# Block sums of two right sides made by accumulating transfers: one Strassen-Winograd trunk layer on one Trainium2 core

## Chip, core and metric

The kernel runs on 1 core of one Trainium2 chip. The metric is the device time of one execution in microseconds (us). TensorE is called PE, VectorE DVE, ScalarE ACT, GpSimd POOL and SyncE SP. POOL and SP also issue the transfers.

## What is computed

One layer of a trunk on 1024 frames of width 1024, all in float32: an input projection, two gated mixers, their two output projections, a third output projection `w_o` into the residual, and a gated feed-forward block.

```python
merged = (sigmoid(gate_a + gate_bias[0]) * (y_a @ w_out_a)
          + sigmoid(gate_b + gate_bias[1]) * (y_b @ w_out_b))
x = x + merged @ w_o
h = rmsnorm(x, ln2_g)
x = x + (silu(h @ w_ffn_gate) * (h @ w_ffn_up)) @ w_ffn_down
return rmsnorm(x, final_g)
```

## The kernel before, in words

**Products.** Every large product is tiled by Strassen-Winograd: a `Pair` is two 128-row output tiles, and its right side is cut into row pairs (two 128-row tiles each, four of them for a width of 1024) and into frame halves H0 and H1 of 512. With a = `y[2q]` and b = `y[2q+1]`, row pair q has the four blocks a.H0 (B11), a.H1 (B12), b.H0 (B21) and b.H1 (B22). Seven products replace eight; each needs a block, or a sum of blocks, of both sides (`PRODS`, line 38). The right sides are called forms: B11, T1 = B11 - B12, T2 = B22 + T1, B21, T3 = B12 - B22, T4 = B21 - T2 and B22.

**Float32 by three products.** Each form, and each left block or sum, is split into a high part, rounded to fp32r by ACT (line 115), and a low part, the rest, by a subtraction on DVE (line 116). Each left-right tile pair is then three matmuls in PE: low by high, high by low, high by high. So a product over four row pairs is 12 matmuls into one PSUM bank.

**Forms.** `form_steps` (line 150) gives the work on the forms of the next stage in seven groups: b11 splits a.H0 and then replaces it by T1 in place (line 159); t1 splits that; t2 adds b.H1 to it (line 168) and splits; b21 splits b.H0 and subtracts T2 from it (line 164); t3 subtracts b.H1 from a.H1 (line 176) and splits; t4 splits b.H0, b22 splits b.H1. That is four DVE operations on 128x512 for a row pair, beside the seven splits. `at_last` (line 333) hangs these groups on the products of a stage's last pair; the row pair 3, whose values come last, is done in the last pair's own evacuation (lines 683 to 687 and 714 to 717).

**The two transitions.** The stage `pa_` (lines 689 to 691) multiplies by `w_out_a`, and its evacuation `ev_oa` makes the merged value: it loads the gate and the other mixer's part through `loaded` (line 651, a POOL transfer of 512 KB each into two buffers), multiplies (line 678) and adds (line 681). Its results `mg` are the right side F4 of the stage `po` (`w_o`, lines 720 to 722). The evacuation `ev_o` there loads x, adds (line 701), scales the sum by `ln2_g` on ACT (line 702) into `h2`, writes x back (line 704) and sums squares; `h2` is the right side F5 of the feed-forward stage `pf`. "First transition" below is from `pa_` to `po`, "second transition" from `po` to `pf`. Row pair 2 is the last one that `at_last` handles, since its evacuation ends while the stage's last pair is being multiplied.

**Order.** Stages with `late=True` (`add_stage`, line 202) begin with P1, P5 and P6 of the first two pairs over row pairs 0 to 2 only, with P4 and P3 of the stage before between them; the row pair 3 follows for both. Every engine runs its instructions in a fixed order, which the scheduler makes from the order of the code and from priorities (evacuations are raised, line 323). The weights come on SP; everything else that is loaded or stored in these stages is issued by POOL, in its order. The left sums are made by DVE (line 252), and PE waits for the splits of the left sides, `ws` (of a sum) and `wa` (of a block as loaded).

Of the kernel before, what the change touches and what calls it, by code (L numbers as in the profile page):

```python
# [8 lines left out]
F32 = mybir.dt.float32  # L9
F32R = mybir.dt.float32r  # L10
AF = mybir.ActivationFunctionType
ALU = mybir.AluOpType

P = 128
T = 1024
D = 1024
KT = D // P
HN = 512
H0, H1 = slice(0, HN), slice(HN, T)
# [12 lines left out]
V_GA, V_GB, V_G1, V_G2, V_GF = 88, 96, 104, 112, 120  # L32
# [18 lines left out]
def trunk(ctx: ExitStack, tc: tile.TileContext, xT, w_first, w_std, w_more, w_in, w_ob, w_oa, w_o, w_gu, wd0, wd1, wd2, w_dl,  # L51
          lru, vec, out):
    nc = tc.nc
    cp = ctx.enter_context(tc.tile_pool(name="cp", bufs=1))
# [49 lines left out]
    sc = cp.tile([P, NV], F32, name="sc")  # L104
# [6 lines left out]
    def col(base, c):  # L111
        return sc[:, base + c : base + c + 1]

    def split(src, hi, lo):
        nc.scalar.activation(hi, src, AF.Copy)  # L115
        nc.vector.tensor_sub(lo, src, hi.bitcast(F32))  # L116
# [30 lines left out]
        nc.vector.scalar_tensor_tensor(R, v, 1.5, y, op0=ALU.add, op1=ALU.mult)  # L147


    def form_steps(y, F, qs):  # L150
        def keep(n, q, src):
            f = form(n.lower())
            split(src, f[:, 0, :], f[:, 1, :])
            F[n][q] = f

        def b11(q):
            a, b = y[2 * q], y[2 * q + 1]
            keep("B11", q, a[:, H0])
            nc.vector.tensor_sub(a[:, H0], a[:, H0], a[:, H1])

        def b21(q):
            a, b = y[2 * q], y[2 * q + 1]
            keep("B21", q, b[:, H0])
            nc.vector.tensor_sub(b[:, H0], b[:, H0], a[:, H0])

        def t2(q):
            a, b = y[2 * q], y[2 * q + 1]
            nc.vector.tensor_add(a[:, H0], b[:, H1], a[:, H0])  # L168
            keep("T2", q, a[:, H0])

        def t1(q):
            keep("T1", q, y[2 * q][:, H0])

        def t3(q):
            a, b = y[2 * q], y[2 * q + 1]
            nc.vector.tensor_sub(a[:, H1], a[:, H1], b[:, H1])
            keep("T3", q, a[:, H1])

        def t4(q):
            keep("T4", q, y[2 * q + 1][:, H0])  # L180

        def b22(q):
            keep("B22", q, y[2 * q + 1][:, H1])

        return [[lambda q=q, f=f: f(q) for q in qs] for f in (b11, t1, t2, b21, t3, t4, b22)]


# [141 lines left out]
    def new_forms(nk=4):  # L329
        return {n: [None] * nk for n in FORMS}  # L330


    def at_last(pair, y, F, qs):
        early = 2 if len(qs) < len(F["B11"]) else 4
        for i, group in enumerate(form_steps(y, F, qs)):
            x = ("P5", "P5", "P2" if early == 2 else "P6", "P2", "P7", "P4", "P3")[i]
            if i < 2:
                group, rest = group[:early], group[early:]
                pair.after.setdefault("P2", []).extend(rest)
            pair.after.setdefault(x, []).extend(group)  # L340
# [212 lines left out]
    for k in range(KT):  # L553
        if k + 2 < KT:
            load_first(k + 2)
        x = xs[k]
# [114 lines left out]
    mg = [None] * KT  # L671
    F4 = new_forms()

    def ev_oa(q):
        def f(t0, t1):
            s = loaded(dsa, 2 * q)
            for i, t in enumerate((t0, t1)):
                nc.vector.tensor_mul(t, t, s[i])
            s = loaded(dmb, 2 * q)
            for i, t in enumerate((t0, t1)):  # L680
                nc.vector.tensor_add(t, t, s[i])
                mg[2 * q + i] = t
            if q == 3:
                for group in form_steps(mg, F4, (3,)):
                    for g in group:
                        g()
        return f

    pa_ = [Pair(w_oa[q], F3, 4, ev_oa(q)) for q in range(4)]
    add_stage(pa_)  # L690
    pa_[-1].before.setdefault("P1", []).append(lambda: at_last(pa_[-1], mg, F4, range(3)))


    F5, h2, S2 = new_forms(), [None] * KT, {}

    def ev_o(q):
        def f(t0, t1):
            xs_ = loaded([xT[m * P : (m + 1) * P, :] for m in range(KT)], 2 * q)
            for i, (t, x) in enumerate(zip((t0, t1), xs_)):
                m = 2 * q + i  # L700
                nc.vector.tensor_add(x, x, t)  # L701
                nc.scalar.activation(t, x, AF.Copy, scale=col(V_G2, m))
                h2[m] = t
                nc.gpsimd.dma_start(dx2[m], x)
                if m == 0:
                    S2[0] = pool["now"].tile([P, T], F32, name="S2")
                for h in (H0, H1):
                    if m == 0:
                        nc.scalar.activation(S2[0][:, h], x[:, h], AF.Square)
                    else:  # L710
                        sq = sum_t("sq")
                        nc.scalar.activation(sq, x[:, h], AF.Square)
                        nc.vector.tensor_add(S2[0][:, h], S2[0][:, h], sq)
            if q == 3:
                for group in form_steps(h2, F5, (3,)):
                    for g in group:
                        g()
        return f

    po = [Pair(w_o[q], F4, 4, ev_o(q)) for q in range(4)]  # L720
    add_stage(po, late=True)
    po[-1].before.setdefault("P1", []).append(lambda: at_last(po[-1], h2, F5, range(3)))


    gs = {}
# [71 lines left out]
    for gi, ((q0, n), w) in enumerate(zip(GROUPS, (wd0, wd1, wd2))):  # L797
        F, y = new_forms(n), [None] * (2 * n)
# [215 lines left out]
```

## Time and profile before

| | us |
|---|---|
| median of 3 runs | 1519.38 |
| lowest, highest | 1517.64, 1519.49 |
| the profiled execution | 1521.04 |
| its span | 1519.3 |
| PE busy in it | 1467.3 (97%) |
| DVE busy | 1163.1 (77%) |
| ACT busy | 855.4 (56%) |
| POOL busy | 142.0 (9%) |

A row of the profile names the line, the engine, the operation and what it writes and reads, without buffer numbers: `ca` and `cb` are the two tiles of a pair's result, `ld` a loaded tile, `b` and `t` forms, `psa`, `psb` and `psc` the PSUM banks of a product. Idle time of an engine is put down to what released it. A matmul of 128x512 that follows others starts 0.227 us after the one before it, so 12 of them take 2.72 us.

### The profile page before, as it was taken

What the parts mean: (1) busy time and instruction counts of PE and PEld (TensorE: products, weight loads), DVE (VectorE), ACT (ScalarE), POOL (GpSimd) and SP (SyncE); (2) the same over time, 40 slices, a digit from 0 to 9 for tenths busy, and PEclk for the clock granted to TensorE, in tenths of its full rate; (3) what the DMA queues carried; (4) which work ended last, traced back from release to release, by engine and by line L of the source; (5) the groups of instructions that cost most, each with busy time, mean ns of one, the idle gap of its engine ahead of it and who ended that gap; (6) DMA issues with size and microseconds to landing.
All of it is one profiled execution on the core that took longest, in us unless ns stands there. A gap on an engine that the chain in (4) does not pass through costs nothing.

```text
span 1519.3 us, 18156 instructions
## 1 busy us (share of the span) xinstructions
PE 1467.3 (97%) x6420; PEld 1199.9 (79%) x6420; DVE 1163.1 (77%) x1713; ACT 855.4 (56%) x1409; POOL 142.0 (9%) x230
## 2 busy tenths in 40 slices
PE   9999999999999999999999899999999999998996
PEld 7787887888878887878777688888888888776885
DVE  7997858768678559698988896666666679888857
ACT  8568759579487447363556654444444445545623
POOL 1301001001010010201001000000000010212100
PEclk9999999999999999999999899999999999998998
DMA  6221221311312363636344132222222243667603
GB/s 223 83 84 56 71 92 46 118 52 44 126 56 77 123 231 106 230 132 216 128 154 165 63 125 83 83 83 83 83 84 83 82 149 112 240 207 262 206 29 111
DMA packets 75915, 181.61 MB, mean 120 GB/s; under 512 B 8352, under 2 KB 18592, under 8 KB 75824
## 3 DMA queue, kind: packets, MB, share of 16 engines
q1 hardware_dynamic: 48000, 83.71, 18.0%
q0 software_dynamic: 26048, 94.45, 17.0%
q10 hardware_dynamic: 1776, 2.29, 0.4%
q8 instruction: 50, 0.82, 0.2%
q14 instruction: 41, 0.34, 0.1%
HBM read 131.14 MB, written 49.28 MB: 119 GB/s over the span
## 4 chain that ended last, share of the span: by engine, by line
PE 76%; DVE 13%; DMA 4%; ACT 4%; issue 3%; POOL 0%; DVEq 0%; ACTq 0%; POOLq 0%
PE psb L124 32%; PE psc L124 21%; PE psa L124 20%; PE psx L124 3%; DVE t L116 2%; DVE ws L116 1%; DMA y<-dmi 1%; DVE s L252 1%; DVE b L116 1%; DVE wa L116 1%; DMA y<-dya 1%; DVE u L379 1%; DVE ca L319 1%; DVE y L168 1%; DVE ld L701 1%
## 5 line engine op out<-in xcount | busy, mean ns | idle before, releaser
L124 PE MATMUL psb<-t,ws 128*128 128x512 f32 x1632 | 405.5, 395 | 13.9 <-DVE ws L116 11.4
L124 PE MATMUL psa<-b,wa 128*128 128x512 f32 x1632 | 397.4, 390 | 3.8 <-ACT b L115 2.5
L124 PEld LDWEIGHTS psb<-t,ws 128*128 128x128 f32 x1632 | 310.1, 191 | 84.3 <-DVE ws L116 13.8
L124 PEld LDWEIGHTS psa<-b,wa 128*128 128x128 f32 x1632 | 305.9, 188 | 70.2 <-ACT b L115 3.7
L116 DVE TENSOR_TENSOR ws<-s,ws 128x512 fp32r<-128x512 f32 (+1 forms) x284 | 188.6, 666 | 85.9 <-ACT ws L115 84.9
L115 ACT ACTIVATE ws<-s 128x512 fp32r<-128x512 f32 (+1 forms) x284 | 171.3, 607 | 136.4 <-DVE s L252 80.4
L124 PE MATMUL psc<-t,ws 128*128 128x512 f32 x816 | 203.1, 396 | 9.6 <-DVE ws L116 5.9
L124 PE MATMUL psb<-t,wa 128*128 128x512 f32 x816 | 200.1, 392 | 3.3 <-DVE wa L116 2.5
L124 PE MATMUL psc<-b,ws 128*128 128x512 f32 x816 | 197.7, 389 | 0.1
L124 PEld LDWEIGHTS psc<-t,ws 128*128 128x128 f32 x816 | 155.0, 191 | 45.2 <-DVE ws L116 6.7
L116 DVE TENSOR_TENSOR wa<-raw,wa 128x512 fp32r<-128x512 f32 (+1 forms) x213 | 142.1, 667 | 56.4 <-ACT wa L115 55.0
L124 PEld LDWEIGHTS psb<-t,wa 128*128 128x128 f32 x816 | 153.7, 189 | 37.3 <-DVE wa L116 3.2
L124 PEld LDWEIGHTS psc<-b,ws 128*128 128x128 f32 x816 | 153.3, 188 | 32.5 <-DVE ws L116 0.6
L115 ACT ACTIVATE wa<-raw 128x512 fp32r<-128x512 f32 (+1 forms) x213 | 128.7, 605 | 61.8 <-issue 52.7
L252 DVE TENSOR_TENSOR s<-raw,raw 128x512 f32<-128x512 f32 (+1 forms) x142 | 93.7, 666 | 25.6 <-DMA raw<-in_w_in 9.1
L252 DVE TENSOR_TENSOR s<-s,raw 128x512 f32<-128x512 f32 (+1 forms) x142 | 94.2, 664 | 1.6
L319 DVE TENSOR_TENSOR ca<-psc,ca 128x512 f32<-128x512 f32 x71 | 48.9, 688 | 35.9 <-PE psc L124 35.7
L291 ACT ACTIVATE psb<-psa 128x512 f32<-128x512 f32 x67 | 38.9, 581 | 64.9 <-PE psa L124 64.8
L294 ACT ACTIVATE cb<-psc 128x512 f32<-128x512 f32 x67 | 39.8, 594 | 60.6 <-PE psc L124 58.7
L299 ACT ACTIVATE ca<-psb 128x512 f32<-128x512 f32 x67 | 39.7, 593 | 52.7 <-PE psb L124 47.3
L304 ACT ACTIVATE ca<-psa 128x512 f32<-128x512 f32 x62 | 36.6, 591 | 46.1 <-PE psa L124 46.0
L317 ACT ACTIVATE cb<-psb 128x512 f32<-128x512 f32 x58 | 34.3, 591 | 45.4 <-PE psb L124 45.3
(251 smaller groups left out, 1591.5 us busy)
## 6 DMA issues: line engine op xcount, KB each, us to landing
raw<-in_w_in SPq DMA_DIRECT2D x100, 256.0 KB, 2.9
raw<-in_w_gu SPq DMA_DIRECT2D x88, 256.0 KB, 2.9
ld<-dx POOLq DMA_DIRECT2D x24, 512.0 KB, 5.5
y<-dmi POOLq DMA_DIRECT2D x22, 512.0 KB, 7.4
raw<-in_wd SPq DMA_DIRECT2D x48, 192.0 KB, 4.0
dmi<-ca POOLq DMA_DIRECT2D x11, 512.0 KB, 2.9
dmi<-cb POOLq DMA_DIRECT2D x11, 512.0 KB, 3.2
ld<-dsb POOLq DMA_DIRECT2D x8, 512.0 KB, 6.3
```

Of the source, the lines that this page charges most:

```text
L115: nc.scalar.activation(hi, src, AF.Copy)
L116: nc.vector.tensor_sub(lo, src, hi.bitcast(F32))
L124: nc.tensor.matmul(o, lhsT=l, rhs=r, start=start, stop=stop, skip_group_check=True)
L168: nc.vector.tensor_add(a[:, H0], b[:, H1], a[:, H0])
L252: nc.vector.tensor_add(t[:, :c], a[:, :c], b[:, :c])
L291: nc.scalar.activation(b["b"], b["a"], AF.Copy, scale=-1.0)
L294: nc.scalar.activation(t1[:, H1], b["c"], AF.Copy)
L299: nc.scalar.activation(t0[:, H1], b["b"], AF.Copy)
L304: nc.scalar.activation(t0[:, H0], b["a"], AF.Copy)
L317: nc.scalar.activation(t1[:, H0], b["b"], AF.Copy)
L319: nc.vector.tensor_sub(t0[:, H1], b["c"], t0[:, H1])
L379: nc.vector.scalar_tensor_tensor(u[:, sh:], src[:, : T - sh], base(k), u[:, sh:], op0=ALU.mult, op1=ALU.add)
```

## The change

In the two transitions, the sums of row pairs 0, 1 and 2 are made by POOL-issued transfers from SBUF to SBUF that add to what stands at their destination. Since a transfer only adds, the evacuations store a.H1 and b.H0 of these row pairs negated, and the splits of B21, T3 and T4 undo the sign (ACT with scale -1, DVE with a scalar-tensor-tensor operation). T3's sum is issued in t1 now. The row pair 3 and all other stages stay as they were.

```diff
-    def form_steps(y, F, qs):
-        def keep(n, q, src):
+    def form_steps(y, F, qs, by_dma=False):
+        def keep(n, q, src, neg=False):
             f = form(n.lower())
-            split(src, f[:, 0, :], f[:, 1, :])
+            if neg:
+                nc.scalar.activation(f[:, 0, :], src, AF.Copy, scale=-1.0)
+                nc.vector.scalar_tensor_tensor(f[:, 1, :], src, -1.0, f[:, 0, :].bitcast(F32), op0=ALU.mult, op1=ALU.subtract)
+            else:
+                split(src, f[:, 0, :], f[:, 1, :])
             F[n][q] = f
+
+        def plus(dst, src):
+            nc.gpsimd.dma_start(dst, src, accum_op=ALU.add)
...
             keep("B11", q, a[:, H0])
-            nc.vector.tensor_sub(a[:, H0], a[:, H0], a[:, H1])
+            if by_dma:
+                plus(a[:, H0], a[:, H1])
+            else:
+                nc.vector.tensor_sub(a[:, H0], a[:, H0], a[:, H1])
...
-            keep("B21", q, b[:, H0])
-            nc.vector.tensor_sub(b[:, H0], b[:, H0], a[:, H0])
+            keep("B21", q, b[:, H0], by_dma)
+            if by_dma:
+                plus(b[:, H0], a[:, H0])
+            else:
+                nc.vector.tensor_sub(b[:, H0], b[:, H0], a[:, H0])
...
         def t1(q):
-            keep("T1", q, y[2 * q][:, H0])
+            a, b = y[2 * q], y[2 * q + 1]
+            keep("T1", q, a[:, H0])
+            if by_dma:
+                plus(a[:, H0], b[:, H1])
+                plus(a[:, H1], b[:, H1])
...
 # ev_oa
-                nc.vector.tensor_add(t, t, s[i])
+                if q == 3:
+                    nc.vector.tensor_add(t, t, s[i])
+                else:
+                    p, n = ((H0, H1), (H1, H0))[i]
+                    nc.vector.tensor_add(t[:, p], t[:, p], s[i][:, p])
+                    nc.vector.scalar_tensor_tensor(t[:, n], t[:, n], -1.0, s[i][:, n], op0=ALU.mult, op1=ALU.subtract)
...
-    pa_[-1].before.setdefault("P1", []).append(lambda: at_last(pa_[-1], mg, F4, range(3)))
+    pa_[-1].before.setdefault("P1", []).append(lambda: at_last(pa_[-1], mg, F4, range(3), True))
...
+    ng2 = cp.tile([P, KT], F32, name="ng2")
+    nc.gpsimd.tensor_scalar(ng2, sc[:, V_G2 : V_G2 + KT], -1.0, None, op0=ALU.mult)
...
 # ev_o
-                nc.scalar.activation(t, x, AF.Copy, scale=col(V_G2, m))
+                if q == 3:
+                    nc.scalar.activation(t, x, AF.Copy, scale=col(V_G2, m))
+                else:
+                    p, n = ((H0, H1), (H1, H0))[i]
+                    nc.scalar.activation(t[:, p], x[:, p], AF.Copy, scale=col(V_G2, m))
+                    nc.scalar.activation(t[:, n], x[:, n], AF.Copy, scale=ng2[:, m : m + 1])
...
-    po[-1].before.setdefault("P1", []).append(lambda: at_last(po[-1], h2, F5, range(3)))
+    po[-1].before.setdefault("P1", []).append(lambda: at_last(po[-1], h2, F5, range(3), True))
```

In the rows of the order below, a name keeps its numbers. DVE in the first transition, from the first operation on row pair 2's T1 on; before:

```order
L159 TENSOR_TENSOR ca939_5786<-ca939_5786 128x512
L116 TENSOR_TENSOR wa11998_6111<-raw967_5952,wa11998_6111 128x512
L176 TENSOR_TENSOR ca939_5786<-ca939_5786,cb940_5787 128x512
L116 TENSOR_TENSOR t1987_6063<-ca939_5786,t1987_6063 128x512
L116 TENSOR_TENSOR t2988_6067<-ca889_5480,t2988_6067 128x512
L116 TENSOR_TENSOR t2989_6071<-ca917_5643,t2989_6071 128x512
L168 TENSOR_TENSOR ca939_5786<-cb940_5787,ca939_5786 128x512
L116 TENSOR_TENSOR t2990_6075<-ca939_5786,t2990_6075 128x512
L678 TENSOR_TENSOR cb962_5930<-cb962_5930,ld1012_6201 128x1024
L116 TENSOR_TENSOR b21991_6078<-cb890_5481,b21991_6078 128x512
L116 TENSOR_TENSOR b21992_6082<-cb918_5644,b21992_6082 128x512
L164 TENSOR_TENSOR cb890_5481<-cb890_5481,ca889_5480 128x512
```

and with the change:

```order
L116 TENSOR_TENSOR wa11998_6122<-raw967_5958,wa11998_6122 128x512
L116 TENSOR_TENSOR t1987_6075<-ca939_5790,t1987_6075 128x512
L116 TENSOR_TENSOR t2988_6080<-ca889_5482,t2988_6080 128x512
L116 TENSOR_TENSOR t2989_6083<-ca917_5645,t2989_6083 128x512
L699 TENSOR_TENSOR cb962_5936<-cb962_5936,ld1012_6209 128x1024
L116 TENSOR_TENSOR t2990_6086<-ca939_5790,t2990_6086 128x512
L157 SCALAR_TENSOR_TENSOR b21991_6089<-cb890_5483,b21991_6089 128x512
L157 SCALAR_TENSOR_TENSOR b21992_6093<-cb918_5646,b21992_6093 128x512
L157 SCALAR_TENSOR_TENSOR b21993_6097<-cb940_5791,b21993_6097 128x512
L157 SCALAR_TENSOR_TENSOR t3999_6125<-ca889_5482,t3999_6125 128x512
L157 SCALAR_TENSOR_TENSOR t31000_6128<-ca917_5645,t31000_6128 128x512
L340 TENSOR_TENSOR ca961_5935<-psc966_5944,ca961_5935 128x512
```

The four kinds of sum are gone from DVE (lines 159, 164, 168 and 176), and row pair 3's multiplication by its gate (line 678, now 699) stands ahead of row pair 2's T2 split instead of behind it.

POOL in the same place, where `ca889` and `cb890` are row pair 0, `ca939` and `cb940` row pair 2; with the change (before, only the six loads through `loaded` stand here):

```order
L675 DMA ld982_6041<-dmb5_112 128x1024
L675 DMA ld1011_6208<-dsa6_81 128x1024
L163 DMA ca939_5790<-ca939_5790 128x512
L675 DMA ld1012_6209<-dsa7_82 128x1024
L163 DMA ca939_5790<-cb940_5791 128x512 x2
L675 DMA ld1013_6214<-dmb6_113 128x1024
L163 DMA cb890_5483<-ca889_5482 128x512
L163 DMA cb918_5646<-ca917_5645 128x512
L163 DMA cb940_5791<-ca939_5790 128x512
L675 DMA ld1014_6215<-dmb7_114 128x1024
```

Row pair 2's four transfers (T1, then T2 and T3, then T4) are issued between the loads for row pair 3, and the three for T4 stand behind the load of `dmb6`.

DVE in the second transition, from the last product P3 of row pair 3's first tile on (`ca1079`); before:

```order
L319 TENSOR_TENSOR ca1079_6618<-psc1084_6627,ca1079_6618 128x512
L164 TENSOR_TENSOR cb1029_6280<-cb1029_6280,ca1028_6279 128x512
L116 TENSOR_TENSOR b211112_6781<-cb1034_6302,b211112_6781 128x512
L116 TENSOR_TENSOR b211113_6785<-cb1056_6466,b211113_6785 128x512
L164 TENSOR_TENSOR cb1034_6302<-cb1034_6302,ca1033_6301 128x512
L164 TENSOR_TENSOR cb1056_6466<-cb1056_6466,ca1055_6465 128x512
L116 TENSOR_TENSOR t31119_6814<-ca1028_6279,t31119_6814 128x512
L116 TENSOR_TENSOR t31120_6818<-ca1033_6301,t31120_6818 128x512
L116 TENSOR_TENSOR t31121_6822<-ca1055_6465,t31121_6822 128x512
L116 TENSOR_TENSOR ws11124_6837<-s1123_6835,ws11124_6837 128x512
L116 TENSOR_TENSOR t41127_6867<-cb1029_6280,t41127_6867 128x512
```

and with the change:

```order
L340 TENSOR_TENSOR ca1079_6630<-psc1084_6639,ca1079_6630 128x512
L116 TENSOR_TENSOR ws11124_6851<-s1123_6849,ws11124_6851 128x512
L729 TENSOR_TENSOR ld1131_6913<-ld1131_6913,ca1079_6630 128x1024
L116 TENSOR_TENSOR t21110_6791<-ca1055_6475,t21110_6791 128x512
L157 SCALAR_TENSOR_TENSOR b211111_6794<-cb1029_6288,b211111_6794 128x512
L157 SCALAR_TENSOR_TENSOR b211112_6798<-cb1034_6310,b211112_6798 128x512
L157 SCALAR_TENSOR_TENSOR b211113_6802<-cb1056_6476,b211113_6802 128x512
L157 SCALAR_TENSOR_TENSOR t31119_6830<-ca1028_6287,t31119_6830 128x512
L157 SCALAR_TENSOR_TENSOR t31120_6833<-ca1033_6309,t31120_6833 128x512
L157 SCALAR_TENSOR_TENSOR t31121_6836<-ca1055_6475,t31121_6836 128x512
L273 TENSOR_TENSOR s1123_6849<-s1123_6849,raw1085_6653 128x512
L157 SCALAR_TENSOR_TENSOR t41127_6881<-cb1029_6288,t41127_6881 128x512
```

The left split `ws11124` and row pair 3's residual add (`ld1131`, line 701, now 729) move ahead of the forms B21 and T3; before, the add came after T4 and a second left split.

## Rows read from the trace of the kernel before

**Rows 1.** Busy time by stretch: start and end, length, PE, PEld, DVE, ACT, POOL, PEclk.

```profile
746.00:770.00 24.00, 18.77 (x75) 13.02 (x74) 22.42 (x34) 12.47 (x23) 2.12 (x4) 1.00 0.29 98
844.80:849.00 4.20, 4.15 (x10) 3.29 (x11) 4.20 (x7) 0.66 (x2) 0.00 (x0) 0.50 0.00 0
```

**Rows 2.** Timeline of PE, first transition: start, length, what, [idle before, releaser].

```profile
752.45 2.20 PE L124 MATMUL psa<-b,wa 128*128 128x512 f32 x9
756.67 2.35 PE L124 MATMUL psc<-t,ws 128*128 128x512 f32 x9 [2.02 <-DVE ws L116]
759.68 2.33 PE L124 MATMUL psb<-t,ws 128*128 128x512 f32 x9 [0.66 <-DVE ws L116]
```

**Rows 3.** Timeline of PE, second transition.

```profile
838.80 2.21 PE L124 MATMUL psa<-b,wa 128*128 128x512 f32 x9
844.85 4.21 PE L124 MATMUL psc<-t,ws 128*128 128x512 f32 x9 [3.83 <-DVE ws L116]
848.85 3.12 PE L124 MATMUL psb<-t,ws 128*128 128x512 f32 x9
868.29 4.17 PE L124 MATMUL psb<-t,wa 128*128 128x512 f32 x11 [2.51 <-DVE wa L116]
873.46 2.90 PE L124 MATMUL psc<-b,ws 128*128 128x512 f32 x12
```

**Rows 4.** Timeline of DVE, first transition.

```profile
740.84 0.69 DVE L116 TENSOR_TENSOR b<-ca,b 128x512 fp32r<-128x512 f32 x1
748.78 1.22 DVE L678 TENSOR_TENSOR cb<-cb,ld 128x1024 f32<-128x1024 f32 x1
751.12 1.28 DVE L164 TENSOR_TENSOR cb<-cb,ca 128x512 f32<-128x512 f32 x2
755.94 0.68 DVE L116 TENSOR_TENSOR ws<-s,ws 128x512 fp32r<-128x512 f32 x1
758.95 0.68 DVE L116 TENSOR_TENSOR ws<-s,ws 128x512 fp32r<-128x512 f32 x1
```

**Rows 5.** Groups of instructions by line and shape: count, busy us, mean ns, idle before.

```profile
L429 DVE SCALAR_TENSOR_TENSOR w<-w,r 128x512 f32<-128x512 f32 x16 | 11.0, 690 | 34.6 <-ACT w L427 34.6
```

**Rows 6.** Transfers by line: count, KB each, median us from issue to landing.

```profile
dsa<-sg POOLq DMA_DIRECT2D x12, 256.0 KB, 2.6
dx<-ld POOLq DMA_DIRECT2D x8, 512.0 KB, 2.9
ld<-in_xT POOLq DMA_DIRECT2D x8, 512.0 KB, 4.3
ld<-dsa POOLq DMA_DIRECT2D x8, 512.0 KB, 4.7
y<-dmi POOLq DMA_DIRECT2D x22, 512.0 KB, 7.4
```

**Rows 7.** Timeline of POOL, both transitions.

```profile
750.29 0.53 POOL L654 DMA_DIRECT2D ld<-dmb  x1 [6.21 <-DVE cb L678]
829.93 0.54 POOL L654 DMA_DIRECT2D ld<-in_xT  x1 [0.92 <-ACT sq L712]
```

**Rows 8.** Timeline of ACT, first transition.

```profile
748.05 0.58 ACT L317 ACTIVATE cb<-psb 128x512 f32<-128x512 f32 x1
```

**Rows 9.** Timeline of DVE, second transition.

```profile
828.89 0.68 DVE L116 TENSOR_TENSOR b<-ca,b 128x512 fp32r<-128x512 f32 x1
833.11 1.89 DVE L116 TENSOR_TENSOR t<-ca,t 128x512 fp32r<-128x512 f32 x3
844.11 0.68 DVE L116 TENSOR_TENSOR ws<-s,ws 128x512 fp32r<-128x512 f32 x1
847.12 0.68 DVE L116 TENSOR_TENSOR ws<-s,ws 128x512 fp32r<-128x512 f32 x1
847.72 1.22 DVE L701 TENSOR_TENSOR ld<-ld,ca 128x1024 f32<-128x1024 f32 x1
850.81 0.69 DVE L116 TENSOR_TENSOR b<-ca,b 128x512 fp32r<-128x512 f32 x1 [1.27 <-ACT b L115]
```

More of the change, by code (lines that the diff above doesn't have):

```diff
@@ L158, in b11 @@
             keep("B11", q, a[:, H0])
-            nc.vector.tensor_sub(a[:, H0], a[:, H0], a[:, H1])
+            if by_dma:
+                plus(a[:, H0], a[:, H1])
+            else:
+                nc.vector.tensor_sub(a[:, H0], a[:, H0], a[:, H1])
         def b21(q):
             a, b = y[2 * q], y[2 * q + 1]
-            keep("B21", q, b[:, H0])
-            nc.vector.tensor_sub(b[:, H0], b[:, H0], a[:, H0])
+            keep("B21", q, b[:, H0], by_dma)
[3 more added lines that the diff above has]
+                nc.vector.tensor_sub(b[:, H0], b[:, H0], a[:, H0])
         def t2(q):
             a, b = y[2 * q], y[2 * q + 1]
-            nc.vector.tensor_add(a[:, H0], b[:, H1], a[:, H0])
+            if not by_dma:
+                nc.vector.tensor_add(a[:, H0], b[:, H1], a[:, H0])
             keep("T2", q, a[:, H0])
         def t1(q):
-            keep("T1", q, y[2 * q][:, H0])
+            a, b = y[2 * q], y[2 * q + 1]
[3 more added lines that the diff above has]
+                plus(a[:, H1], b[:, H1])
         def t3(q):
             a, b = y[2 * q], y[2 * q + 1]
-            nc.vector.tensor_sub(a[:, H1], a[:, H1], b[:, H1])
-            keep("T3", q, a[:, H1])
+            if not by_dma:
+                nc.vector.tensor_sub(a[:, H1], a[:, H1], b[:, H1])
+            keep("T3", q, a[:, H1], by_dma)
         def t4(q):
-            keep("T4", q, y[2 * q + 1][:, H0])
+            keep("T4", q, y[2 * q + 1][:, H0], by_dma)
         def b22(q):
@@ L330, in new_forms, with at_last @@
         return {n: [None] * nk for n in FORMS}
-    def at_last(pair, y, F, qs):
+    def at_last(pair, y, F, qs, by_dma=False):
         early = 2 if len(qs) < len(F["B11"]) else 4
-        for i, group in enumerate(form_steps(y, F, qs)):
+        for i, group in enumerate(form_steps(y, F, qs, by_dma)):
             x = ("P5", "P5", "P2" if early == 2 else "P6", "P2", "P7", "P4", "P3")[i]
```

## The prediction

> **What bounds the kernel now.** The page's totals come first: PE is busy for 97% of the span, so the change, which leaves every matmul as it is, can only win or lose time where PE stands still or runs slowly. The busy times by stretch show where that is. In the 24 us around the first transition PE is busy for 18.8 us and DVE for 22.4, and at the second one there is a stretch at a granted clock of 0.50, the 1.2 GHz level [rows 1]. PE's timeline names the waits: 2.02 and 0.66 us for DVE's `ws` in the first transition [rows 2], 3.83 us for a `ws` and 2.51 for a `wa` in the second [rows 3]. There the cost is larger than the idle time, since the nine matmuls behind the 3.83 us took 4.21 us where nine before it took 2.21. DVE's timeline tells why the weight splits are late: they stand in order behind the sums of blocks and the forms, back to back at 0.60 us each (a pair of sums, 1.28 us) [rows 4]. So DVE is the bound in both transitions, and the change takes work from DVE. The question is what it puts in its place.
>
> **What goes and what comes, on the engines.** For each row pair four DVE sums go: 12 in a transition, 12 x 0.60 = 7.2 us, 14.4 in both. The additions of line 681 are cut into halves: 1.28 us for two instead of 1.22, six times, 0.4 us. B21, T3 and T4 are split by a scalar-tensor-tensor, which at 128x512 takes 0.69 us [rows 5], as a subtraction does: nothing. ACT's two half scalings and its scale of -1 I take as nothing as well. POOL gets 24 issues of some 0.53 us [rows 7], 12.7 us, and waits most of the time anyway; the negation of `ln2_g` lies at the start, where POOL is free.
>
> **The unknown.** Call D the time from the issue of one adding transfer (256 KB, SBUF to SBUF) to its landing. No row shows one. Nearest are POOL's stores: 256 KB in 2.6 us, 512 KB in 2.9 [rows 6]. An adding transfer reads two operands of 256 KB and writes one, so I take 2.9 and, for the third 256 KB, the 0.3 between those rows: D = 3.2. The lower end is the store, 2.6; upper ends are the single loads of these stages, 4.3 and 4.7, and the loads queued eight at a time, 7.4. D counts several times over, because each row pair's sums form a chain: T1, then T2 and T3 from it, then T4.
>
> **First transition.** Row pair 2 decides. The split of its B11 starts at 740.84 now [rows 4]; a left sum moves behind it, so it ends at about 741.0. Issue (0.1 after), landing, ACT's copy 0.62 and DVE's split 0.69 put T1 at 742.4 + D; the transfer for T2 and ACT's copy of it end at 743.1 + 2D. DVE's order has row pair 3's multiplication (line 699) ahead of that split. It needs ACT's copy of P4's bank, which PE delivers for 748.05 [rows 8]; now that copy need not queue behind T2's. It starts at about 748.3 and ends at 749.5. With D = 3.2, 743.1 + 6.4 = 749.5: T2 is just in time. Nine DVE operations of 0.60 follow up to the first `ws`: 754.9, where it ended at 756.6 before. Meanwhile T4's first transfer, issued after B21's split (749.5 + 1.2 + 0.1 = 750.8; the `dmb` load [rows 7] goes just ahead of it on POOL), lands at 754.0 and is copied by 754.6: not late. Five more operations put the second `ws` at 757.9 against 759.6. Gain 1.7, less 0.1 for the halved additions: **1.6 us**. A smaller D brings nothing more, since P4 sets the 749.5. A larger one costs three times over: at D = 4 T2 starts at 751.1, T4's copy is there at 757.0, the `ws` at 760.0, a loss of 0.4; at 4.7 the loss is 2.5, at 6 it is 6.4.
>
> **Second transition.** B11's split of row pair 2 ends at 829.6 [rows 9]. Its T1 transfer goes behind an x load that POOL issues at 829.93 [rows 7] and that takes 4.3 us [rows 6]: both land at about 834.3. T1 is split at 835.6, against 833.8 now: 1.8 us are lost here, of which PE feels about one, in the last products of the old stage. But P3 still ends at 838.2 to 838.8 [rows 3], and behind it DVE now has only the bank's read, the `ws` (839.4 instead of 844.8) and row pair 3's residual add, done at 840.6; it started at 847.72 [rows 9]. The 3.83 us wait goes. Next is T2 (its transfer landed at 838.9), B21, and the first T4 transfer from 841.9 to 845.1, copied by 845.7; DVE fills the time with six operations up to 845.4. The `ws` for P6 is done at 846.9 (847.8 before), so PE's stall moves there from P5, about 4 us long, and may again be followed by slow matmuls. The split of row pair 3's B11 ends at 848.7 instead of 851.5 [rows 9]. From there DVE's order stays the bound: 12 operations and two ACT copies (about 1 us) to P2's `wa`, 856.9, six more to P7's `ws`, 860.5. Four products and the four small sums then need 11.8 us behind the later of 860.5 and P2's end, which is 859.6 at full rate and 862.5 at the slow rate of [rows 3]: 872.3 to 874.3, against 876.3 now (873.46 and 2.90). Between 2.0 and 4.0 I take the 2.8 us by which the chain is ahead, less 0.2 for halves: **2.6 us**. Each us of D above 3.2 costs one here (T4's transfer), and three from about 4.4 on, where T2 is late too; below 3.0 DVE is the bound and nothing more comes.
>
> **Sum.** 1.6 + 2.6 = 4.2 us off the profiled execution's 1521.04: 1516.8. The three timed runs have their median 1.66 us lower, so 1519.38 - 4.2 = **1515.2**.
>
> **A rule against it.** POOL's issues stay at 0.53 us beside a DVE that is busy almost throughout [rows 1, 7]; if each had instead to sit out a DVE operation of 0.69 us [rows 5], D would be 3.9 and the sum -0.1 + 1.9 = 1.8 us, 1517.6. The Trainium skill (SBUF — State Buffer, Summary: rules for kernel authors) advises against hiding a POOL-issued transfer under a DVE operation, because descriptors can't be written while DVE holds the shared port in its faster modes. By that rule the 1517.6 would hold; by the rows it doesn't, as the operations here are of the same kind as those beside the 0.53.
>
> **Rivals.** First, *no change that can be told* (0.2%, 3.0 us): D between 3.55 and 4.9, from the crowding that the loads in these stages show (4.3 and 4.7), or from stretched issues. At D = 4.3 the transitions give -1.3 + 1.5 = 0.2: 1519.2; the band is 1516.4 to 1522.4. For it: the new transfers share POOL's queue with 512 KB loads. Against: stores from SBUF, more alike, take 2.9 in the same stages. Second, *slower*: the three transfers in a row take the place of DVE as the bound. It decides from D = 4.9; if the addition makes a transfer twice as long as a store, D = 6, the losses are 6.4 and 3.4, 9.8 in all: 1529.2, and PE's longer waits would bring more of the slow clock. For it: each form waits for the one before and POOL, ACT and DVE take their work in a fixed order, so one late T2 holds row pair 3 and the weights. Against: only that T2 and T4 have some 6 us of other work to hide in. Third, that the freed DVE time isn't used (another wait ends last): 1519.4, inside the first; the rows of DVE's back-to-back work speak against it.
>
> **Chances.** Forecast 0.46, no change 0.32, slower 0.22. The gain ends at 4.4 us however short D is; with 2.3 us for what such sums miss, above all the slow matmuls, the low end is 1512.5. The high end is D = 4.9 and a little: 1523.0. That leaves out most of the last rival and little below.
>
> **What would show it.** Right: adding transfers landing in about 3.2 us, no wait of PE for `ws` near 844, row pair 3's residual add near 840 instead of 847.72, the first `ws` in the first transition near 755. Wrong: ACT waiting for T2 or T4 transfers by more than 1 us, DVE idle behind it, and the waits of PE on `ws` as long as now or longer. A landing of 4.5 us or more would overturn the forecast.

## The result: 14.2 us slower

The changed kernel took 1533.3 us (median of 4 runs, 1533.1 to 1536.95) beside 1519.12 for the kernel before (4 runs on the same chip, 1517.64 to 1519.49). The ratio is 1.0095, with a 95% interval of 1.0083 to 1.0108: slower, and outside the predicted range. Its profiled execution took 1536.95 us, with a span of 1535.2; the one of before 1521.04 and 1519.3.

The page's totals after:

```profile
PE 1469.8 (96%) x6420; PEld 1200.2 (78%) x6420; DVE 1150.1 (75%) x1695; ACT 856.1 (56%) x1415; POOL 163.4 (11%) x255
```

DVE's busy time fell by 13.0 us (1163.1 before), as planned, and PE did the same matmuls. PE waits longer. The timeline of PE after, with its waits, and the rows that serve as marks below:

```profile
734.62 2.88 PE L124 MATMUL psa<-b,wa 128*128 128x512 f32 x12
744.04 0.49 PE L124 MATMUL psa<-b,wa 128*128 128x512 f32 x1 [2.46 <-ACT b L115]
765.01 3.07 PE L124 MATMUL psb<-t,ws 128*128 128x512 f32 x9 [2.06 <-DVE ws L116]
778.50 2.88 PE L124 MATMUL psb<-t,ws 128*128 128x512 f32 x12
831.42 4.52 PE L124 MATMUL psb<-t,ws 128*128 128x512 f32 x12 [3.60 <-ACT ca L320]
849.59 0.79 PE L124 MATMUL psc<-t,ws 128*128 128x512 f32 x1 [3.88 <-ACT t L115]
864.97 3.88 PE L124 MATMUL psb<-t,ws 128*128 128x512 f32 x9 [4.52 <-DVE ws L116]
892.03 2.88 PE L124 MATMUL psb<-t,ws 128*128 128x512 f32 x12
```

The same three marks in the timeline of PE before:

```profile
735.12 2.88 PE L124 MATMUL psa<-b,wa 128*128 128x512 f32 x12
772.87 2.88 PE L124 MATMUL psb<-t,ws 128*128 128x512 f32 x12
876.20 2.88 PE L124 MATMUL psb<-t,ws 128*128 128x512 f32 x12
```

From the first mark to the second lies the first transition: 43.88 us after, 37.75 before, so 6.1 are lost. From the second to the third lies the second: 113.53 against 103.33, so 10.2. Together that is 16.3, the whole difference of the profiled executions (15.9) within half a us. The waits for `ws` in [rows 2, 3] did not go; new ones stand beside them, for B11 (744.04), for a bank's copy (831.42) and for T1 (849.59). The stretch at the 1.2 GHz level [rows 1] is there again, behind the wait for T1:

```profile
849.60:854.00 4.40, 4.40 (x10) 3.46 (x11) 2.47 (x4) 2.64 (x4) 2.17 (x3) 0.50 0.72 186
```

(us, then busy us and count of PE, PEld, DVE, ACT and POOL, granted clock, DMA share, GB/s.)

The adding transfers themselves: their groups in the DMA view from 690 to 920 us (count, KB each, median us to landing), and two lines of the view of their source line:

```profile
ca<-cb POOLq DMA_DIRECT2D x12, 256.0 KB, 3.5
ca<-ca POOLq DMA_DIRECT2D x6, 256.0 KB, 7.2
cb<-ca POOLq DMA_DIRECT2D x6, 256.0 KB, 4.4
```

```profile
L163 POOL DMA_DIRECT2D ca<-ca x6: 887/904/1227, 724.8 to 841.3; - x6
...
DMA to landing us min/median/max: 3.3/4.7/8.4
```

The fastest, 3.3 us, is the forecast's 3.2; the median is 4.7, and T1's (`ca<-ca`) is 7.2. An issue takes POOL 0.9 us, not the 0.53 of [rows 7].

**Where the first transition's time goes** can be followed through four engines, and it starts ahead of row pair 2. Timeline of ACT, before and after, at T1 of row pairs 0 and 1:

```profile
728.17 0.62 ACT L115 ACTIVATE t<-ca 128x512 fp32r<-128x512 f32 x1
729.88 0.60 ACT L317 ACTIVATE cb<-psb 128x512 f32<-128x512 f32 x1 [1.08 <-PE psb L124]
```

```profile
729.91 0.63 ACT L115 ACTIVATE t<-ca 128x512 fp32r<-128x512 f32 x1 [2.14 <-DMA ca<-ca]
732.27 0.63 ACT L115 ACTIVATE t<-ca 128x512 fp32r<-128x512 f32 x1 [1.73 <-DMA ca<-ca]
732.81 0.58 ACT L338 ACTIVATE cb<-psb 128x512 f32<-128x512 f32 x1
```

Before, ACT had copied both T1s by the time that PE delivered P4's bank of row pair 2's tiles, and read it at once (L317). After, it stands in its order at two T1s that have not landed, and reads the bank (L338) at 732.81. DVE, which splits the same T1s, stands in its order too: its multiplication of that tile follows its second T1 split without a gap, and the bank read had ended 0.2 us earlier. So both orders hold it back, and with it everything that leads to row pair 2's B11. Timeline of DVE before, then after:

```profile
730.98 1.22 DVE L678 TENSOR_TENSOR cb<-cb,ld 128x1024 f32<-128x1024 f32 x1
...
738.38 1.22 DVE L681 TENSOR_TENSOR ca<-ca,ld 128x1024 f32<-128x1024 f32 x1
```

```profile
732.94 0.69 DVE L116 TENSOR_TENSOR t<-ca,t 128x512 fp32r<-128x512 f32 x1 [1.67 <-ACT t L115]
733.55 1.22 DVE L699 TENSOR_TENSOR cb<-cb,ld 128x1024 f32<-128x1024 f32 x1
...
742.63 0.69 DVE L706 TENSOR_TENSOR ca<-ca,ld 128x512 f32<-128x512 f32 x1 [3.00 <-DMA ld<-dmb]
...
744.44 0.68 DVE L116 TENSOR_TENSOR b<-ca,b 128x512 fp32r<-128x512 f32 x1
```

The multiplication frees the buffer that the `dmb` load waits for. POOL's timeline before, then after:

```profile
732.49 0.53 POOL L654 DMA_DIRECT2D ld<-dmb  x1 [7.83 <-DVE cb L678]
```

```profile
732.53 2.67 POOL L163 DMA_DIRECT2D ca<-cb  x3 [1.50 <-DMA ca<-ca]
735.07 0.70 POOL L675 DMA_DIRECT2D ld<-dmb  x1
```

So the load goes 2.6 us later. It also takes longer. The view of the tile `dmb`, for this one transfer alone, before and then after, where the three additions were issued just ahead of it:

```profile
DMA to landing us min/median/max: 3.5/3.5/3.5
DMA to landing us min/median/max: 7.5/7.5/7.5
```

DVE waits 3.00 us for it, from 739.63 on; with the 3.5 us of before it would have landed at about 738.6 (an estimate, 735.07 + 3.5), ahead of DVE. So the wait takes both, the late issue and the slow landing. B11 of row pair 2 is split at 744.44 where [rows 4] had 740.84: 9.8 us behind the first mark in place of 5.7. The prediction had the chain of row pair 2 begin on time, and loads that land as before.

**In the second transition** it is the same wait, longer. Timeline of ACT after:

```profile
827.02 0.63 ACT L115 ACTIVATE t<-ca 128x512 fp32r<-128x512 f32 x1 [6.93 <-DMA ca<-ca]
827.56 0.58 ACT L338 ACTIVATE cb<-psb 128x512 f32<-128x512 f32 x1
...
830.79 0.57 ACT L320 ACTIVATE ca<-psb 128x512 f32<-128x512 f32 x1
...
848.91 1.67 ACT L115 ACTIVATE t<-ca 128x512 fp32r<-128x512 f32 x3 [4.16 <-DMA ca<-ca]
...
856.92 0.63 ACT L115 ACTIVATE t<-ca 128x512 fp32r<-128x512 f32 x1 [4.19 <-DMA ca<-cb]
```

T1 of row pair 0, issued with the next at 819.33, keeps ACT idle for 6.93 us. Two bank reads stand behind it, and PE needs the second (the 3.60 us at 831.42). Later come 4.16 us for T1 of row pair 2 and 4.19 for its T2, and DVE stands 4.26 us for an x load (at 847.11). What the prediction named as signs of being wrong is there: ACT's wait for a T2, PE's waits for `ws` of 2.06 and 4.52 us, and a landing above 4.5 us in the median.

### The profile page after: what moved, and what is told of

It is laid out like the page before. It is cut to its first block, busy times and chain, and to the rows that moved or that the text cites. A ratio compares the mean times of both kernels' runs of the same rounds, so it can differ in the third digit from the quotient of the medians.

```text
span 1535.2 us, 18201 instructions
## 1 busy us (share of the span) xinstructions
PE 1469.8 (96%) x6420; PEld 1200.2 (78%) x6420; DVE 1150.1 (75%) x1695; ACT 856.1 (56%) x1415; POOL 163.4 (11%) x255
## 3 DMA queue, kind: packets, MB, share of 16 engines
q0 software_dynamic: 29504, 100.74, 19.3%
## 4 chain that ended last, share of the span: by engine, by line
PE 69%; DVE 15%; DMA 7%; ACT 4%; issue 3%; POOL 1%; DVEq 0%; POOLq 0%; ACTq 0%
PE psb L124 29%; PE psc L124 19%; PE psa L124 19%; PE psx L124 2%; DVE t L116 2%; DVE ws L116 2%; DMA ca<-ca 1%; DVE s L273 1%; DVE b L116 1%; DMA y<-dmi 1%; DVE wa L116 1%; DVE u L400 1%; DMA cb<-ca 1%; DVE x L631 1%; DVE y L184 1%
## 5 line engine op out<-in xcount | busy, mean ns | idle before, releaser
L124 PE MATMUL psb<-t,ws 128*128 128x512 f32 x1632 | 410.1, 398 | 28.2 <-DVE ws L116 18.9
L338 ACT ACTIVATE cb<-psb 128x512 f32<-128x512 f32 x58 | 34.3, 592 | 50.0 <-PE psb L124 50.0
```

Source lines behind the costliest of these rows:

```text
L124: nc.tensor.matmul(o, lhsT=l, rhs=r, start=start, stop=stop, skip_group_check=True)
L338: nc.scalar.activation(t1[:, H0], b["b"], AF.Copy)
```

## The experiments

Each kernel was timed against the kernel before on the same chip. "First" and "second" are the us by which the stretches between the three marks are longer than before, from one profiled execution of each. One execution says little about the second transition (8b, level by its ratio, stands 2.7 us off there), so the ratios decide. Transfers and sums below are always those of row pairs 0, 1 and 2.

| | kernel | ratio (95%) | first | second |
|---|---|---|---|---|
| | the change | 1.0095 (1.0083 to 1.0108) | +6.1 | +10.2 |
| 1 | all sums back on DVE, signs kept | 1.0008 (0.9993 to 1.0022) | +0.1 | +1.7 |
| 2 | first transition only | 1.0043 (1.0030 to 1.0056) | +6.3 | -0.7 |
| 3 | second transition only | 1.0054 (1.0035 to 1.0074) | 0.0 | +8.8 |
| 4 | copies in place of additions | 1.0025 (1.0013 to 1.0038) | +0.3 | +3.8 |
| 5 | transfers for row pairs 0, 1 | 1.0062 (1.0042 to 1.0081) | +3.6 | +1.0 |
| 6 | transfers for row pair 2 | 1.0052 (1.0032 to 1.0072) | +1.7 | +2.6 |
| 7 | T3, T4 by transfers | 0.9998 (0.9982 to 1.0013) | -0.7 | 0.0 |
| 8 | the change, loads on SP | 1.0096 (1.0072 to 1.0119) | +5.5 | +10.2 |
| 8b | before, loads on SP | 0.9994 (0.9980 to 1.0007) | 0.0 | -2.7 |
| 9 | T3 computed by POOL | 1.0016 (1.0001 to 1.0030) | +1.3 | +1.9 |
| 10 | T3, T4 computed by POOL | 1.0037 (1.0023 to 1.0050) | +2.9 | +2.7 |
| 11 | sums left out | 0.9976 (0.9962 to 0.9990) | 0.0 | -4.1 |
| 12 | T2, T3, T4 by transfers | 1.0023 (1.0012 to 1.0033) | +1.5 | +1.1 |
| 13 | T1 of row pairs 0, 1 and T2 later | 1.0085 (1.0066 to 1.0103) | +4.0 | +5.2 |
| 14 | T3 by transfers | 1.0012 (1.0001 to 1.0022) | -0.5 | +1.8 |
| 15 | T1 by transfers | 1.0107 (1.0092 to 1.0122) | +7.5 | +5.1 |
| 16 | the change, T1 of row pair 2 on DVE | 1.0084 (1.0067 to 1.0101) | +5.6 | +4.8 |

**1. Signs.**

```diff
         def plus(dst, src):
-            nc.gpsimd.dma_start(dst, src, accum_op=ALU.add)
+            nc.vector.tensor_add(dst, dst, src)
```

> The change with its negated halves and split scalings kept, but each of the 24 sums is a DVE addition of 128x512 again, in the place in the code where the transfer stood. Theory (the transfers cost the time: their landings and what stands behind them): back at the kernel before, 1519 to 1520.5 us, since only 0.4 us of halved additions and some ACT halves are left. Rival (the cost is in the signs: halved additions, ACT's scalings by halves and by -1, and the scalar-tensor-tensor splits on DVE): stays at 1528 to 1533.

1.0008: the halves and signs cost nothing that can be told (3 us at most, by the interval). The loss is the transfers'.

**2 and 3. One transition each.** `at_last` called without `True`, and the signs of that evacuation as before:

```diff
-    po[-1].before.setdefault("P1", []).append(lambda: at_last(po[-1], h2, F5, range(3), True))
+    po[-1].before.setdefault("P1", []).append(lambda: at_last(po[-1], h2, F5, range(3)))
```

> Transfers and signs in the first transition only; the second as before. In the two traces the first row of 12 matmuls behind the first transition came 6.1 us later against the one ahead of it. Theory (the two transitions lose independently, 6 and 10): 1524 to 1526. Rival (a part of the second's loss is passed on from the first, through queues and buffers that are late): 1520 to 1523 here and the more in the second alone.

> Transfers and signs in the second transition only; the first as before. Theory (independent losses; 10.2 us behind the second transition in the two traces, 1.7 of it the profiled execution's own distance from the median): 1527.5 to 1530. Rival (passed on from the first): 1530 to 1533 here, or the time of before plus less than 5, depending on which way it is passed.

0.43% and 0.54% are 6.5 and 8.2 us, 14.7 together where the change lost 14.4: the two losses add up, as far as intervals of 2 to 3 us either way can tell.

**4. Copies.**

```diff
-            nc.gpsimd.dma_start(dst, src, accum_op=ALU.add)
+            nc.gpsimd.dma_start(dst, src)
```

> The change with the same 24 transfers at the same places, as plain copies without the addition, so T1 to T4 of row pairs 0, 1 and 2 hold a copied block in place of a sum. Theory A (an adding transfer is long because it adds): SBUF to SBUF copies land in 2.6 to 3.3 us, POOL's issue is back at 0.53, the time falls to 1515 to 1524. Theory B (the order of POOL's queue and of ACT and DVE behind any transfer): landings shorten by less than 1 us and the time stays at 1528 to 1533.

The loss falls to 0.25%, 3.8 us. The same view of the line, for the copies:

```profile
L163 POOL DMA_DIRECT2D ca<-ca x6: 541/541/541, 725.0 to 833.7; - x6
...
DMA to landing us min/median/max: 2.2/2.9/6.4
```

Theory A holds on issue and time: some 10 of the 14 us are there because the transfers add. The landings spread to 6.4 us all the same, and in the second transition ACT still waits 5.62 us for the copy in the place of row pair 0's T1 (PE then 1.59 us for a bank's copy).

**The price by itself.**

> A kernel that only measures transfers; none of the reference is computed in it. Each in SBUF with nothing beside it: single additions and copies of 256 KB, three in a row of each, 512 KB of each, then one of each beside six loads of 512 KB, and beside a DVE that is busy with 128x512 subtractions. Theory A (an addition costs much more than a copy, by itself): single addition 3.3 us or more and copy 2.2 to 2.6, POOL's issue 0.9 and 0.53, three additions land 1.3 us or more apart and copies well under 1. Theory C (crowding by loads makes the landings long): single addition 2.6 to 3, like a copy, and over 4 only beside the loads. If the DVE's work stretches POOL's issue, 0.9 beside the subtractions and 0.5 without.

From the timeline of POOL (issues), and of DVE, which reads each result as soon as it has landed:

```profile
24.51 0.87 POOL L74 DMA_DIRECT2D t<-t  x1 [8.06 <-DVE t L69]
...
33.76 0.57 POOL L77 DMA_DIRECT2D t<-t  x1 [3.81 <-DVE t L69]
...
44.66 2.66 POOL L74 DMA_DIRECT2D t<-t  x3 [3.02 <-DVE t L69]
...
142.05 0.89 POOL L74 DMA_DIRECT2D t<-t  x1 [14.30 <-DVE t L69]
```

```profile
27.91 0.69 DVE L67 TENSOR_TENSOR g<-g,t 128x512 f32<-128x512 f32 x1 [3.30 <-DMA t<-t]
...
36.11 0.69 DVE L67 TENSOR_TENSOR g<-g,t 128x512 f32<-128x512 f32 x1 [2.35 <-DMA t<-t]
...
48.11 0.69 DVE L67 TENSOR_TENSOR g<-g,t 128x512 f32<-128x512 f32 x1 [3.33 <-DMA t<-t]
49.62 0.69 DVE L67 TENSOR_TENSOR g<-g,t 128x512 f32<-128x512 f32 x1 [0.82 <-DMA t<-t]
51.00 0.69 DVE L67 TENSOR_TENSOR g<-g,t 128x512 f32<-128x512 f32 x1 [0.69 <-DMA t<-t]
...
108.75 0.69 DVE L67 TENSOR_TENSOR g<-g,t 128x512 f32<-128x512 f32 x1 [8.24 <-DMA t<-t]
...
145.33 0.69 DVE L67 TENSOR_TENSOR g<-g,t 128x512 f32<-128x512 f32 x1 [0.63 <-DMA t<-t]
```

A single addition (24.51 to 27.91) is there after 3.4 us, a copy (33.76 to 36.11) after 2.35. Three additions in a row come 1.5 and 1.4 us apart (49.62, 51.00). Beside six loads of 512 KB an addition took 8.4 us (issued at 100.39, read at 108.75), copies 7.1 and 6.7. Beside DVE's subtractions (142.05) nothing changed: 0.89 for the issue, 3.3 to the landing. So A holds: an addition costs 1 us more than a copy by itself. Of C one half falls (by itself an addition is not like a copy) and the other holds: the loads add 5 us to an addition and 4.3 to 4.8 to a copy. The 0.9 us issue is the addition's, not DVE's doing.

**5 and 6. By row pairs.** `plus` takes q, and the rest goes to DVE; 5 has `q < 2`, 6 has `q == 2`:

```diff
+            if q < 2:
                 nc.gpsimd.dma_start(dst, src, accum_op=ALU.add)
+            else:
+                nc.vector.tensor_add(dst, dst, src)
```

> Signs as in the change; the sums of row pairs 0 and 1 by transfers, those of row pair 2 on DVE. Theory B (head of the line: loads stand behind these transfers on POOL, and ACT and DVE wait for them in order ahead of evacuations that PE needs, the 2.46 and 3.60 us waits of PE in the changed kernel): at least 5 of the 14 us are here, ratio to the kernel before 1.003 to 1.006. Theory A (only the chain of row pair 2 costs): 1.000 to 1.001.

> Signs as in the change; the sums of row pair 2 by transfers, those of row pairs 0 and 1 on DVE. Theory A (the chain of row pair 2 costs what the landings of its three transfers in a row make): ratio 1.005 to 1.009. Theory B (the transfers ahead of it cost the most): 1.001 to 1.004.

Both lose, 9.4 and 7.9 us by the ratios. Row pairs 0 and 1, which the prediction costed at nothing, cost at least as much as row pair 2. In 5, B11 of row pair 2 comes 9.1 us behind the first mark (5.7 before), in 6 only 5.1. But 6 alone loses too, although its eight transfers landed in 3.2 to 5.2 us, median 3.5: from 725 to 900 us ACT waits 9.3 us there for T1s and T2s and 5.8 for T4s.

**7, 12, 14 and 15. By link of the chain.** `plus` is told the number of the form that the sum makes, here as q, and DVE makes the others:

```diff
-        def plus(dst, src):
-            nc.gpsimd.dma_start(dst, src, accum_op=ALU.add)
+        def plus(q, dst, src):
+            if q in (3, 4):
+                nc.gpsimd.dma_start(dst, src, accum_op=ALU.add)
+            else:
+                nc.vector.tensor_add(dst, dst, src)
```

That is 7; 12 has `(2, 3, 4)` and 15 `(1,)`. 14 has T3 alone, with only a.H1 negated.

> Signs as in the change; T1 and T2 on DVE, only T3 and T4 by transfers, for row pairs 0, 1 and 2. Then no transfer waits for another and a form has one transfer ahead of it at most. Theory A and B alike (what costs is that T2's transfer can only be issued when T1's has landed and has been split, and that POOL waits there): most of the loss goes, ratio 0.998 to 1.002; if 6 of 12 sums off DVE then bring what was forecast, 0.998. Rival (any adding transfer beside the loads costs, whatever waits for it): 1.004 or more.

> Signs as in the change; T1 on DVE, T2, T3 and T4 by transfers, for row pairs 0, 1 and 2: the first of the three transfers in a row goes, 18 of 24 stay. Theory A (each link of the chain costs by ACT's and DVE's wait for its landing, in their order): much of the loss goes, ratio 1.001 to 1.004. Rival (the number of transfers in POOL's queue at 1.4 us each sets the loss): three quarters stay, 1.006 to 1.008.

> Only T3's sums of row pairs 0, 1 and 2 by transfers (only a.H1 negated), the others on DVE as before: each transfer has other forms between it and its use, none waits for another. If DVE time counts: 3 x 0.60 less 0.2 in each transition, 1516 to 1517.5, ratio 0.998. Rival (as without sums, the freed time isn't used): 1.000 within 0.001.

> Signs as in the change; only T1 by transfers, T2, T3 and T4 on DVE, for row pairs 0, 1 and 2: 6 of 24 transfers, none of which has another ahead of it in its chain, so POOL waits for no landing. Theory A1 (T1's own landing is what ACT, DVE and PE wait for): most of the 11 us by which the kernel with T2, T3 and T4 is better than the change shows here, ratio 1.005 to 1.008. Theory A2 (T1's landing costs through what stands behind it, POOL's wait and the later transfers at 1.4 us each): 1.001 to 1.003.

T3 and T4 by transfers come out level with before, and T3 alone does not gain either (1.0012): the forecast's 0.998 for both was missed, though no engine waits for a transfer in 14. T4's are still late in the first transition of 7, where DVE waits 1.83 us behind ACT for the third of them. T2 beside T3 and T4 costs 3.8 us (1.0023 less 0.9998), T1 beside all three another 11 (1.0095 less 1.0023). T1 alone costs as much as the whole change, above what was expected of A1. That settles A1 against A2: POOL waits for no sum in kernel 15, and only 6 transfers are left, 2 in a row at most. ACT's waits there, from 700 to 900 us (total, times, longest), and PE's from 725 to 900:

```profile
ACT t L115 <- DMA ca<-ca: 19.3, 6, 5.7
```

```profile
PE psa L124 <- ACT b L115: 12.5, 4, 4.7
```

ACT waits 19.3 us for T1 in its order, and PE 12.5 us for B11s that come late (2.5 before). DVE, which makes T2 from T1 there, waits another 7.6 us for T1's landing in its own order, so kernel 15 does not tell the two engines' orders apart. In 12, with T1 on DVE, the load for row pair 2 took 6.9 us beside T2 and T3, but was issued sooner: DVE waited 0.54 us, and B11 came 5.7 us behind the first mark, as before.

**8 and 8b. Loads on SP.** `loaded` of `ev_oa` and `ev_o` issues on SP, in the change and in the kernel before:

```diff
-    def loaded(src, c0):
+    def loaded(src, c0, eng=None):
...
-            nc.gpsimd.dma_start(t, src[c0 + i])
+            (eng or nc.gpsimd).dma_start(t, src[c0 + i])
...
-            s = loaded(dsa, 2 * q)
+            s = loaded(dsa, 2 * q, nc.sync)
```

(The loads of `dmb` and of x get `nc.sync` in the same way.)

> The change with the loads of ev_oa and ev_o (gates, the other mixer's part, x) issued by SP in place of POOL, so that they no longer stand behind the adding transfers. Theory B (a good part of the loss is loads that stand behind transfers, and behind POOL's wait for T1's landing): 1521 to 1527, or at least 5 us better against the next kernel than the change is against the kernel before. Theory A with ACT's and DVE's order (the transfers' own pace, 1.4 us each, and three in a row): within 3 us of the change, 1530 to 1536.

> The kernel before with the same loads issued by SP, as the other side of the comparison. Both theories: 1517 to 1522; if SP's wait for a free buffer holds up the weights behind it, more, and then the kernel with transfers has to be held against this one.

1.0096 against 0.9994: nothing comes back. Theory B, loads that stand behind the transfers on POOL's queue, falls as the account of the loss. In 8 row pair 2's load is issued as soon as its buffer is free and lands after 6.0 us, and its B11 comes 7.5 us behind the first mark in place of 9.8. But the stretch is only 0.6 us shorter: PE now waits 2.68 us for T1 of row pair 2.

**9 and 10. Sums on POOL.**

```diff
-            nc.vector.tensor_sub(a[:, H1], a[:, H1], b[:, H1])
+            ge.tensor_sub(a[:, H1], a[:, H1], b[:, H1])
```

(`ge` is `nc.gpsimd` in the two transitions and `nc.vector` elsewhere; 10 does the same for T4.)

> The kernel before with T3's sums of row pairs 0, 1 and 2 in both transitions computed by POOL itself, as a 128x512 subtraction, where the trace shows 1.75 us for one on POOL: no signs and no transfer. DVE loses 3 x 0.60 in each transition. If freed DVE time counts where nothing new is waited for: 1516 to 1518. Rival (POOL's 5.2 us hold the loads behind them, or its work slows DVE's): 1519 to 1523.

> As the last one, T4's sums on POOL too: DVE loses 6 x 0.60 in each transition, POOL gets 10.5 us. If freed DVE time counts: 1514 to 1517. Rival (T4 is in a chain behind B21 and T2, and three of 1.75 in a row are later than three of 0.60 on DVE): 1518 to 1523.

Both lose, 2.4 and 5.6 us, at 1.67 to 1.71 us (median) for a subtraction on POOL; one in 9 shows 8.2. The rival named the right side, for 10 by too little (1524.71 against 1518 to 1523); which of its reasons holds was not tested.

**11. No sums.** The four lines (159, 164, 168 and 176) are skipped in both transitions:

```diff
-            nc.vector.tensor_sub(a[:, H0], a[:, H0], a[:, H1])
+            if not free:
+                nc.vector.tensor_sub(a[:, H0], a[:, H0], a[:, H1])
```

> The kernel before with the 24 sums of row pairs 0, 1 and 2 left out and nothing in their place (T1 to T4 of these row pairs hold single blocks): the most that taking the sums off DVE can give. The prediction's own sum has 4.4 us with the shortest transfers: 1515, ratio 0.997. Rival (the freed DVE time isn't used, another wait ends last): 1518 to 1520, ratio 0.999 or more.

0.9976, so 3.6 us: about what the prediction had for the shortest transfers, but all of it in the second transition. In the first nothing comes of it. Its PE and DVE show why:

```profile
758.75 0.73 PE L124 MATMUL psa<-b,wa 128*128 128x512 f32 x2 [2.65 <-ACT b L115]
```

```profile
751.12 0.67 DVE L116 TENSOR_TENSOR ws<-s,ws 128x512 fp32r<-128x512 f32 x1
...
756.81 1.23 DVE L685 TENSOR_TENSOR ca<-ca,ld 128x1024 f32<-128x1024 f32 x1 [2.14 <-DMA ld<-dmb]
```

The second `ws` is ready at 751.8, 19.0 us behind the first mark (732.82 here), where it was 24.5 behind before [rows 4]. Then DVE waits for the `dmb` load of row pair 3, and PE for B11 of that row pair. The wait for `ws` has only changed its name.

**13. Later forms.**

```diff
-            if i < 2:
+            if by_dma and 0 < i < 3:
+                x = ("P2", "P7")[i - 1]
+            elif i < 2:
```

> The change with the forms T1 of row pairs 0 and 1 made two products later (behind P2 in place of P5) and T2 of all one product later, so that their transfers have 2.7 to 5.4 us more before ACT comes to them. Theory A' (the loss of row pairs 0 and 1 is ACT standing in its order at a T1 that has not landed, 6.9 us in the second transition, with P4's evacuation behind it that PE waits 3.6 us for): that wait goes, 1524 to 1529. Rival (the landings themselves are late whatever the order, and row pair 2 and the weights set the end): 1530 to 1535; and if the forms then come too late for the next stage's P5, more.

1.0085, 1531.89 us: the range of theory A' (1524 to 1529) was missed, and the rival's (1530 to 1535) was met. By the ratio 1.5 us come back, within the noise; by the profiled execution, the fastest of its four, 7. In the second transition ACT reads P4's bank 7.7 us sooner behind the second mark (816.93 and 775.59 here), but in the first the wait is now one for T2, with the same kind of bank read behind it. Timeline of ACT:

```profile
751.70 0.63 ACT L115 ACTIVATE t<-ca 128x512 fp32r<-128x512 f32 x1 [3.34 <-DMA ca<-cb]
752.24 0.58 ACT L338 ACTIVATE cb<-psb 128x512 f32<-128x512 f32 x1
```

**16. Row pair 2's T1 back on DVE.**

```diff
-            if by_dma:
+            if by_dma and q < 2:
                 plus(a[:, H0], a[:, H1])
+            elif by_dma:
+                nc.vector.tensor_add(a[:, H0], a[:, H0], a[:, H1])
```

> The change with one sum in each transition back on DVE: T1 of row pair 2. The prediction's view (the chain of row pair 2 decides, the others cost nothing): at least 7 of the 14 us come back, ratio 1.001 to 1.005. Rival (the chains of row pairs 0 and 1 cost as much, through the one queue and ACT's order): 1.006 to 1.009.

1.0084: 1.7 us of 14 come back, within the noise, while T1 of all three row pairs on DVE (12) gives back 11. So the T1s of row pairs 0 and 1 account for some 9 us of the change's loss (1.0084 less 1.0023), as long as T2 to T4 are transfers too.

## Why the prediction was wrong

- **What bounds the kernel** was read rightly: PE loses where it waits, in the two transitions. DVE as the bound holds for the second one (11: 4 us). In the first it does not: of the forecast's 1.6 us there nothing came even without sums, since the loads of row pair 3 take their place (11). The third rival (the freed time isn't used), which was set aside because DVE's rows stand back to back, was right in that place.
- **The cost of signs and halves**, nothing to 0.4 us: kernel 1 shows no other (1.0008, up to 1.0022).
- **D = 3.2** was right for a single addition with nothing beside it: 3.4 measured, 3.3 the shortest in the kernel. In place it was 4.7 in the median and 7.2 for T1. What failed is the step that took D from single stores: the transfers come two and three in a row, 1.4 us apart, and beside loads. The text's own limit, that a landing of 4.5 us or more would overturn the forecast, was passed.
- **"Row pair 2 decides"**, with the transfers of row pairs 0 and 1 costed at nothing, is the step that failed worst. ACT comes to their T1 up to 6.9 us before it lands, and what stands behind it in ACT's order, and in DVE's behind its split, waits: bank reads, and in the first transition the multiplication that frees the buffer of row pair 2's load. That row pair's own chain starts 4.1 us late there (9.8 against 5.7 us behind the mark). Kernels 12 and 16 show what these T1s cost beside T2 to T4, some 9 of the 14 us, and in 15 the T1s of all three row pairs cost as much as the whole change. How they cost it is read from the traces; the kernel aimed at ACT's order (13) missed its range. Row pair 2's transfers lose by themselves too (6). The prediction asked what is queued behind the transfer on POOL and never what is queued behind ACT's and DVE's wait for it.
- **Loads that land as before** was assumed without a word: beside three additions the load for row pair 2's B11 took 7.5 us in place of 3.5. By itself that costs little (12); on top of the late issue it made DVE's 3.00 us wait.
- **"P3 still ends at 838.2 to 838.8"** fell with that, since P4's and P6's banks were read late, and P3's last matmuls stood in PE's order behind the wait for T1 at 849.59.
- **POOL's 12.7 us of issues at no cost**: the issues take 0.9 us, not 0.53, but POOL's queue is not where the time went (8, 15).
- **The slower rival** named the right side and the right kind, transfers in a row as the new bound, and a size (1529.2) 4 us short; its condition (D from 4.9) was met by T1's 7.2. It placed the cost in T2 and T4 of row pair 2, where T1 of the other two carries it.
- **The rule against it** (the Trainium skill, SBUF — State Buffer, Summary: rules for kernel authors) is not seen here: issues took 0.89 us beside a busy DVE and 0.87 beside an idle one. Both figures are from the kernel of prices, whose DVE made float32 subtractions of 128x512; other kinds of operation were not measured by themselves.
- **The low end**, 1512.5, is 0.2 us below what its own terms give (1519.4 - 4.4 - 2.3); nothing hangs on it.

Left open: why two additions come 1.4 us apart; how much of T1's 7.2 us in place is loads and how much the additions ahead of it (row pair 0's T1, with no addition ahead, took 5.1 us in the first transition and 7.7 in the second, so other traffic is a good part); how much is ACT's order and how much DVE's; and the split between row pairs, since 5 and 6 add up to 17 us by their ratios and to 9 by their profiled executions (13 and 15 differ too, by 4 us each). None of the kernels that compute the whole reference was shown to be faster than the kernel before.

## What to carry to other kernels

When an operation of an engine becomes a transfer, its latency grows from 0.6 us to 3.3 or more, and the engines that read the result stand in their order until it lands: look first at what is queued behind those reads, above all PSUM reads, and move only sums that have other work between issue and use (T3 and T4 here, which cost nothing that can be told, and gained nothing). Measure a transfer as often in a row and beside the same loads as it will run, and look at what it does to those loads. Leave the freed operations out altogether once: that shows in one kernel whether there is anything to gain.

## What was not expected of the hardware

A transfer that adds is dearer than a copy in every part: POOL's issue 0.87 us against 0.57, the landing of 256 KB 3.4 against 2.35, and 1.4 to 1.5 us between landings of three in a row. For 512 KB it is 4.6 (issued at 70.36, read at 75.00) against 3.0 (82.69, 85.70). From 735 to 775 us the DMA engines' busy share was 0.68 in the change and 0.35 before, and a 512 KB load issued there behind three additions took 7.5 us to land, 3.5 before.
